# The last down projection of 256 tokens with tokens on partitions, normalised by bn_stats, its last 512 features in two PSUM tiles

## The chip, the cores and the metric

The kernel runs on one core of a Trainium2 chip. The metric is device time in microseconds from launch to end, taken as the median of several runs; three runs of the kernel before gave 1087.12, 1089.46 and 1090.7. One more execution was profiled, and every single duration below is from it.

A core has five engines with a queue of instructions each: TensorE (PE, with its weight loads shown as PEld), VectorE (DVE), ScalarE (ACT), GpSimd (POOL) and SyncE (SP, which here only issues DMAs). SBUF and PSUM have 128 partitions; TensorE writes PSUM alone, in banks of 512 fp32 values per partition.

## The reference

One layer of a hybrid trunk for 512 prompt tokens and 8 x 4 sample tokens, 544 in all, with 1024 features:

```
x = layer_norm(ALPHA * x + 0.5 * swiglu(x, ffn1), ln1)
proj = x @ w_in ; RWKV-7 heads and a short convolution ; mix = [y_rwkv, y_conv] @ w_out
x = layer_norm(ALPHA * x + mix, ln2)
y = layer_norm(ALPHA * x + 0.5 * swiglu(x, ffn2), ln3)

swiglu(x, wg, wu, wd) = (silu(x @ wg) * (x @ wu)) @ wd
layer_norm(x, g, b)   = (x - mean) * rsqrt(var + 1e-5) * g + b      # over the 1024 features
```

The hidden width of swiglu is 2816, which is 22 rows of 128. Only the very last line, the down projection `@ wd` of the second swiglu and its layer norm `ln3`, is touched by the change.

## The kernel before

**Layout.** Activations stand with features on partitions: `z` is 128 x 8 x 544, where `z[:, d]` holds features 128 d to 128 d + 127 of all tokens. `HALF` splits the tokens into 0 to 255 and 256 to 543. `z` holds ALPHA * x and collects the projection, so that it is the input of the norm (the residual and the products are doubled, and epsilon times four).

**Products.** Every factor is split into a high part in fp32r and a low part (the rest), and each product is three matmuls: high x high, high x low, low x high (`mm3`, L150 to L152). Weights are loaded by SP into a ring of `raw` tiles and split by ScalarE (L134) and VectorE (L135) into a ring of `hl` tiles (`wload`, `wsplit`); late in the kernel there are five raw tiles, six hl tiles and four half-size `hlb` tiles. PSUM has three banks named `mm` (`big()`) and five named `sm`.

**The second swiglu (`f2`).** The hidden rows are worked in `CHUNKS` of 4, 4, 4, 4 and 6. For all but the last chunk a Strassen-like scheme is used in both directions (`pairs`, `downs`, L547 to L549). The last chunk's six rows of hidden activations lie in `hhl` (high and low parts, 6 x 544), and its down projection is plain: `down(LAST, d, h)` computes the 128 features `d` for the tokens of half `h` from six weight blocks, adds the PSUM tile to `z` (L427), and adds the row into a running sum `s1` for the mean (`add_sum`). `main()` ends with the eight `down`s of the second half (288 tokens); their weights stay in SBUF, and `end()` is the eight `down`s of the first half (256 tokens) with the same weights.

**The end.** `layer_norm` of the second half is woven with `end()`: `weave` lets the norm, at each of its yields, hand a number of nanoseconds of matmul work to the other generator, scaled by `FILL["l3a"]`. The norm takes mean and variance over partitions with matmuls against a matrix of ones (L222), subtracts (L235), squares (L236), takes Ln and Exp on ScalarE (L255, L258), multiplies (L262), and applies gain and bias (L268). Once the first half's products are done, `layer_norm_end` normalises those 256 tokens in the same layout, in two groups of 128 tokens, and stores pairs of features as they come (lines L275 to L304). Nothing runs beside it.

**Order.** The program is written as generators; the framework's planner then orders each engine's instructions by the program's order and by when its own model thinks that they are ready, and puts in the waits. `tc.issue_after(x)` puts an instruction behind `x` in its engine's queue. Each engine's queue is in order on the chip, SP's too.

Of the kernel before, what the change touches and what calls it, by code (L numbers as in the profile page):

```python
# [12 lines left out]
F32 = mybir.dt.float32  # L13
F32R = mybir.dt.float32r
AF = mybir.ActivationFunctionType
OP = mybir.AluOpType
# [3 lines left out]
P = 128  # L20
D = 1024
KD = D // P
# [3 lines left out]
NSEQ = 8  # L26
TS = 4
T = TP + NSEQ * TS
B11, B21, B22, NT1, NT2, T3, T4 = range(7)
HALF = ((0, 256), (256, 544))  # L30
# [5 lines left out]
CHUNKS = ((0, 4), (4, 8), (8, 12), (12, 16), (16, 22))  # L36
LAST = len(CHUNKS) - 1
# [21 lines left out]


@with_exitstack
def body(ctx: ExitStack, tc: tile.TileContext, xT, gu1, wd1, win, wo_c, wo_0, wo_1, gu2, wd2, lora, vec, cst,
         sst, cstate, s0, y_o, wkvp_o, wkvs_o, shift_o, conv_o):
    nc = tc.nc
    PE, ACT, DVE, POOL = nc.tensor, nc.scalar, nc.vector, nc.gpsimd
    dma = nc.sync.dma_start

    def pool(st, name, side="left", **kw):
        return st.enter_context(tc.tile_pool(name=name, bufs=1, side=side, reuse_waits="tile", **kw))

    keep = pool(ctx, "keep")
    wp = pool(ctx, "wp")
# [14 lines left out]
    def col(v, i):  # L87
        return vc[:, v + i:v + i + 1]
# [4 lines left out]
    def sm():  # L93
        return ps.tile([P, 512], F32, name="sm", bufs=5)
# [105 lines left out]
    def weave(key, crit, *fill):  # L200
        bg.extend(fill)
        for need in crit:
            take(need * FILL[key])

    def drain(*fill):
        bg.extend(fill)
        take(1e9)
# [5 lines left out]
    def layer_norm(z, c0, c1, gcol, bcol, epsv, q, rs, s1, sink, table=None, hl2=None, both=False):  # L213
        n = c1 - c0
        pair = hl2 is None

        def mean_of(x, need):
            split(hl2[:, 0, :n], hl2[:, 1, :n], x)
            o = sm()
            yield need  # L220
            for i in range(2):
                PE.matmul(o[:, :n], onr, hl2[:, i, :n], start=(i == 0), stop=(i == 1))  # L222
            return o

        if pair:
            m = sm()
            PE.matmul(m[:, :n], ones, s1[:, :n], start=True, stop=False)
            PE.matmul(m[:, :n], ones, z[:, KD - 1, c0:c1], start=False, stop=True)
        else:
            m = yield from mean_of(s1[:, :n], 1300)  # L230
        yield 800 if pair else 300
        for j in range(4):
            zz = z[:, 2 * j:2 * j + 2, c0:c1]
            qq = q[:, 2 * j:2 * j + 2, :n]
            DVE.tensor_tensor(zz, zz, m[:, None, :n].to_broadcast([P, 2, n]), op=OP.subtract)  # L235
            sq = ACT.activation(qq, zz, AF.Square)  # L236
            if j == 0 and table == "ahead":
                tab = issue(sq, ACT.preload_act_table_set, "natural_log_exp_and_others")
            if pair:
                if j % 2:  # L240
                    DVE.tensor_tensor(q[:, 2 * j - 2:2 * j, :n], q[:, 2 * j - 2:2 * j, :n], qq, op=OP.add)
            elif j:
                DVE.tensor_tensor(q[:, 0:2, :n], q[:, 0:2, :n], qq, op=OP.add)
            yield 900 if pair else 1000
        if pair:
            v = sm()
            for i, j in enumerate((0, 1, 4, 5)):
                PE.matmul(v[:, :n], ones, q[:, j, :n], start=(i == 0), stop=(i == 3))
        else:
            DVE.tensor_tensor(q[:, 0, :n], q[:, 0, :n], q[:, 1, :n], op=OP.add)  # L250
            v = yield from mean_of(q[:, 0, :n], 900)
        yield 800 if pair else 600
        if table == "late":
            tab = issue(ACT.activation(warm, v[:, 0:1], AF.Copy), ACT.preload_act_table_set, "natural_log_exp_and_others")
        ln = ACT.activation(rs[:, :n], v[:, :n], AF.Ln, bias=epsv)  # L255
        if table:
            after(ln, tab)
        ACT.activation(rs[:, :n], rs[:, :n], AF.Exp, scale=-0.5)  # L258
        yield 1200 if pair else 600
        for d in range(0, KD, 2):  # L260
            zz = z[:, d:d + 2, c0:c1]
            DVE.tensor_tensor(zz, zz, rs[:, None, :n].to_broadcast([P, 2, n]), op=OP.mult)  # L262
            for e in (d, d + 1):
                x, g, b = z[:, e, c0:c1], col(gcol, e), col(bcol, e)
                if both and e > d:
                    DVE.tensor_scalar(x, x, g, b, op0=OP.mult, op1=OP.add)
                else:
                    ACT.activation(x, x, AF.Identity, scale=g, bias=b)  # L268
            sink(d, zz, c0, c1)
            yield 1600 if pair else 1700  # L270

    def layer_norm_end(z, gcol, bcol, epsv, q, rs, s1):

        m, o = sm(), sm()
        PE.matmul(m[:, :256], ones, s1[:, :256], start=True, stop=False)  # L275
        PE.matmul(m[:, :256], ones, z[:, KD - 1, 0:256], start=False, stop=True)
        for _ in range(3):
            PE.matmul(o[:, :256], ones, s1[:, :256], start=True, stop=True)
        cs = [slice(0, P), slice(P, 2 * P)]

        def two(x):
            return x[:, None, :].to_broadcast([P, 2, P])

        for c in cs:
            v = sm()
            for j in range(0, KD, 2):
                zz, qq = z[:, j:j + 2, c], q[:, j:j + 2, c]
                DVE.tensor_tensor(zz, zz, two(m[:, c]), op=OP.subtract)
                ACT.activation(qq, zz, AF.Square)
                for i in range(2):  # L290
                    PE.matmul(v[:, :P], ones, qq[:, i, :], start=(j + i == 0), stop=(j + i == KD - 1))
            ACT.activation(rs[:, c], v[:, :P], AF.Ln, bias=epsv)
            ACT.activation(rs[:, c], rs[:, c], AF.Exp, scale=-0.5)
        for n, c in enumerate(cs):
            for d in range(0, KD, 2):
                zz = z[:, d:d + 2, c]
                DVE.tensor_tensor(zz, zz, two(rs[:, c]), op=OP.mult)
                for e in (d, d + 1):
                    x, g, b = z[:, e, c], col(gcol, e), col(bcol, e)
                    if e % 2 or e == 6:  # L300
                        DVE.tensor_scalar(x, x, g, b, op0=OP.mult, op1=OP.add)
                    else:
                        ACT.activation(x, x, AF.Identity, scale=g, bias=b)
                dma(y_o[:, d:d + 2, c], zz)  # L304
        yield 0

    def to_x(spill):
        def sink(d, x, c0, c1):
# [3 lines left out]
        return sink  # L312

    def to_y(d, x, c0, c1):
        dma(y_o[:, d:d + 2, c0:c1], x)

    def add_sum(s1, z, d, c0, c1, top):
        n = c1 - c0
# [5 lines left out]
    class Ffn:  # L324
# [21 lines left out]

        def open_lnq(self):
            self.tst.close()
            return pool(self.tst, "lnq" + self.ph).tile([P, KD, 288], F32, name="lnq")

        def weights(self, key, src, n, pair=False):
            if key not in self.w:
# [313 lines left out]
        def main(self):  # L666
            self.open_tv()
            tv = self.inputs()
            self.raw, self.held, self.t = {}, [], 0
            self.todo, self.events = self.plan()  # L670
            z = self.z
            self.done, self.made = set(), set()
            for i, m in enumerate((3, 0, 1, 2) if self.nf > NEX else range(self.na)):
                if m >= self.nf:
                    yield from self.up(m, 0)
                yield from self.up(m, 1)
                next(tv)
                if i == 1 and self.nf < self.na:
                    for j, n in enumerate("gu"):
                        self.w[n, 3] = wload(self.gu[3, :, j, :])  # L680
                elif i in (1, 2):
                    self.t = (-12, -5)[i - 1]
                    self.feed()
            self.t = 0
            for _ in tv:
                pass
            for d in range(KD):
                ACT.activation(z[:, d], z[:, d], AF.Copy, scale=2.0 * ALPHA)
            for ci in range(LAST + 1):
                if ci:  # L690
                    yield from self.pairs(ci)
                if ci < LAST:
                    yield from self.downs(ci)
            for d in range(KD):
                yield from self.down(LAST, d, 1 - self.late)

        def end(self):
            return seq(*(self.down(LAST, d, self.late) for d in range(KD)))
# [780 lines left out]
    weave("l2b", ln2b, f2.first())  # L1479
    drain(f2.main())  # L1480
    lnq = f2.open_lnq()
    weave("l3a", layer_norm(z, *HALF[1], V_LN3G, V_LN3B, epsf, lnq, f2.lnr, f2.s1[1], to_y, "ahead", f2.hl2), f2.end())
    drain()
    drain(layer_norm_end(z, V_LN3G, V_LN3B, epsf, lnq, f2.lnr, f2.s1[0]))
    f2.close()


# [3 lines left out]
def _constants():  # L1491
# [15 lines left out]
    return c  # L1507


_OUTS = [("y", (P, KD, T)), ("wkvp", (P, 4, 64)), ("wkvs", (P, 4, NSEQ, 64)), ("shift", (P, 14, 9)),  # L1510
         ("conv", (P, 4, 2 + 2 * NSEQ))]


# [52 lines left out]
```

## Time and profile before

| what | us |
|---|---|
| median of three runs | 1089.46 |
| profiled execution, its own time | 1087.86 |
| its span, first to last instruction | 1086.1 |
| down rows of the last 288 tokens, from about | 1035.5 to 1054.3 |
| down rows of the first 256 tokens | 1054.3 to 1072.5 |
| normalisation of the first 256 tokens | 1072.5 to 1083.2 |
| last store, to the end of the span | 1083.2 to 1086.1 |

In the rows of the profile, times are microseconds from the start of the span. A row of a group has the line, engine, operation, output <- inputs, shapes and count, then busy time and the mean nanoseconds of one, then the idle time of the engine ahead of it and what ended that. A row of the timeline has start, length, engine, line and instruction. Matmuls are pipelined: what one costs is the distance between two starts, and not its length, which holds the way through the array too.

### The profile page before, as it was taken

How to read it: one execution, taken by the hardware profiler on the slowest of the kernel's cores; microseconds unless marked ns; L12 is line 12 of the kernel's file. 1: busy time of each engine (PE TensorE's matmuls, PEld its weight loads, DVE VectorE, ACT ScalarE, POOL GpSimd, SP SyncE). 2: the span in 40 equal slices, each digit the busy share in tenths (PEclk: the TensorE clock that was granted, in tenths of full speed). 3: DMA queues.
4: the chain of work that ended last, by engine and by line, in shares of the span. 5: the costliest groups of instructions: out<-in, count | busy, mean ns of one | idle time of the engine just before them, and what ended most of it. 6: DMA issues, size and time to landing. Idle time of an engine off the chain costs nothing.

```text
span 1086.1 us, 22868 instructions
## 1 busy us (share of the span) xinstructions
PE 1057.3 (97%) x9258; PEld 1018.5 (94%) x9258; DVE 846.2 (78%) x1576; ACT 588.7 (54%) x1095; POOL 177.5 (16%) x288
## 2 busy tenths in 40 slices
PE   9999999999999999999999999999999999999997
PEld 8999999999999988898889987999999999999996
DVE  7788888889675867775578558999889888888657
ACT  6655565555553677653445334667555565545425
POOL 0122220312200022141001200001312213121000
PEclk9999999999999999999999999999999999999999
DMA  8668595867854233243145625343857859677402
GB/s 280 138 124 191 121 217 132 177 156 148 187 117 154 80 114 84 59 111 85 42 141 185 146 78 178 117 136 78 184 152 153 196 119 211 154 156 177 122 1 83
DMA packets 99081, 148.88 MB, mean 137 GB/s; under 512 B 35232, under 2 KB 60576, under 8 KB 98976
## 3 DMA queue, kind: packets, MB, share of 16 engines
q1 hardware_dynamic: 71776, 111.25, 33.4%
q0 software_dynamic: 27200, 36.18, 22.0%
q8 instruction: 72, 1.18, 0.4%
q14 instruction: 33, 0.27, 0.1%
HBM read 128.74 MB, written 9.75 MB: 128 GB/s over the span
## 4 chain that ended last, share of the span: by engine, by line
PE 67%; issue 10%; DVE 9%; ACT 7%; DMA 6%; SPq 0%; POOL 0%; DVEq 0%; POOLq 0%; ACTq 0%
PE mm L150 7%; PE mm L547 7%; PE mm L151 7%; PE mm L548 7%; PE mm L549 7%; PE mm L152 7%; PE sm L549 5%; PE sm L548 5%; PE sm L547 5%; DMA raw<-in_gu 4%; ACT hl L134 3%; DVE hl L135 2%; PE sm L1047 1%; PE sm L150 1%; PE sm L151 1%
## 5 line engine op out<-in xcount | busy, mean ns | idle before, releaser
L135 DVE TENSOR_TENSOR hl<-raw,hl 128x1024 fp32r<-128x1024 f32 (+3 forms) x232 | 270.6, 1171 | 76.7 <-ACT hl L134 75.6
L134 ACT ACTIVATE hl<-raw 128x1024 fp32r<-128x1024 f32 (+3 forms) x232 | 232.0, 1013 | 90.4 <-DVE raw L514 40.9
L150 PE MATMUL mm<-xhl,hl 128*128 128x288 f32 (+1 forms) x736 | 218.8, 298 | 3.2 <-DVE z L1438 1.6
L151 PE MATMUL mm<-xhl,hl 128*128 128x288 f32 (+1 forms) x736 | 212.9, 289 | 0.3 <-DVE xhl L139 0.3
L152 PE MATMUL mm<-xhl,hl 128*128 128x288 f32 (+1 forms) x736 | 211.5, 288 | 0.1
L150 PEld LDWEIGHTS mm<-xhl,hl 128*128 128x128 f32 x736 | 138.0, 188 | 10.2 <-DVE z L1438 2.6
L151 PEld LDWEIGHTS mm<-xhl,hl 128*128 128x128 f32 x736 | 138.3, 188 | 2.5 <-issue 1.0
L152 PEld LDWEIGHTS mm<-xhl,hl 128*128 128x128 f32 x736 | 138.3, 188 | 1.1 <-DVE hl L135 0.5
L549 PE MATMUL sm<-xhl,hl 128*128 128x272 f32 x432 | 125.3, 290 | 0.0
L548 PE MATMUL sm<-xhl,hl 128*128 128x272 f32 x432 | 124.5, 288 | 0.0
L547 PE MATMUL sm<-xhl,hl 128*128 128x272 f32 x432 | 124.0, 287 | 0.0
L547 PE MATMUL mm<-tv,hl 128*128 128x272 f32 x288 | 83.3, 289 | 3.8 <-ACT cpb L608 2.0
L520 POOL DMA_DIRECT2D raw<-in_gu x36 | 43.4, 1206 | 258.1 <-DVE hlb L139 156.6
L549 PE MATMUL mm<-tv,hl 128*128 128x272 f32 x288 | 83.4, 290 | 0.0
L548 PE MATMUL mm<-tv,hl 128*128 128x272 f32 x288 | 83.1, 289 | 0.0
L547 PEld LDWEIGHTS sm<-xhl,hl 128*128 128x128 f32 x432 | 81.4, 188 | 0.0
L549 PEld LDWEIGHTS sm<-xhl,hl 128*128 128x128 f32 x432 | 81.3, 188 | 0.0
L548 PEld LDWEIGHTS sm<-xhl,hl 128*128 128x128 f32 x432 | 81.2, 188 | 0.0
L526 POOL DMA_DIRECT2D raw<-in_wd x32 | 39.3, 1481 | 249.1 <-DVE hlb L139 218.1
L547 PEld LDWEIGHTS mm<-tv,hl 128*128 128x128 f32 x288 | 54.3, 188 | 5.2 <-ACT cpb L608 3.1
L547 PE MATMUL mm<-hhl,hl 128*128 128x272 f32 x192 | 57.0, 302 | 0.7 <-DVE z L637 0.7
L547 PE MATMUL sm<-hhl,hl 128*128 128x272 f32 x192 | 55.9, 291 | 0.0
(393 smaller groups left out, 2785.5 us busy)
## 6 DMA issues: line engine op xcount, KB each, us to landing
raw<-in_gu SPq DMA_DIRECT2D x84, 512.0 KB, 4.6
raw<-in_gu POOLq DMA_DIRECT2D x36, 512.0 KB, 6.3
raw<-in_wd SPq DMA_DIRECT2D x32, 512.0 KB, 4.7
raw<-in_win SPq DMA_DIRECT2D x26, 512.0 KB, 3.7
raw<-in_wd POOLq DMA_DIRECT2D x32, 256.0 KB, 7.1
raw<-in_wd SPq DMA_DIRECT2D x16, 384.0 KB, 3.2
z<-cpb POOLq DMA_DIRECT2D x16, 272.0 KB, 9.4
z<-sv POOLq DMA_DIRECT2D x16, 272.0 KB, 6.5
```

Source lines behind the costliest of these rows:

```text
L134: ACT.activation(hl[:, 0, a:b], raw[:, a:b], AF.Copy)
L135: DVE.tensor_tensor(hl[:, 1, a:b], raw[:, a:b], hl[:, 0, a:b].bitcast(F32), op=OP.subtract)
L150: PE.matmul(out, wh, src[:, 0, k, c0:c1], start=(start and i == 0), stop=False)
L151: PE.matmul(out, wh, src[:, 1, k, c0:c1], start=False, stop=False)
L152: seen["fill"] = PE.matmul(out, wl, src[:, 0, k, c0:c1], start=False, stop=(stop and i == n - 1))
L520: POOL.dma_start(x.rearrange("p (s c) -> p s c", s=2), bass.AP(tensor=a11.tensor, offset=a11.offset, ap=[[2 * D, P], [P * 2 * D, 2], [1, 5 ...
L526: POOL.dma_start(four(x)[:, i], bass.AP(tensor=a11.tensor, offset=a11.offset, ap=[[DFF, P], [P * DFF, 2], [1, 256]]), accum_op=OP.add)
L547: PE.matmul(out, wh, src(0, i), start=(first and i == 0), stop=False, skip_group_check=True)
L548: PE.matmul(out, wh, src(1, i), start=False, stop=False, skip_group_check=True)
L549: PE.matmul(out, wl, src(0, i), start=False, stop=(i == n - 1), skip_group_check=True)
L1047: crit(PE.matmul(q[r0:r0 + m, o:o + nn], lhs, rhs, start=True, stop=True))
```

## The change

The down projection of the last six hidden rows is done in another layout for the first 256 tokens, and the norm of these tokens with it.

- The weights of the last chunk come as six tiles `wl[m]` of 128 hidden features x 1024 output features (512 KB each), in place of eight tiles of 128 x 768 (384 KB each).
- `down_wide` replaces the eight `down`s of the second half in `main()`: the same matmuls, of 288 columns; for the first four features rows the loop over `m` is the outer one and four PSUM tiles are open at once, for the other four rows it is as before. The split of the tiles from `m` = 4 on is queued behind the planner's held instructions.
- `end_wide` replaces `end()`. For each 128 tokens, `z` is transposed by TensorE into PSUM (eight transposes of 128 x 128 in fp32), and the products are added onto it with the activations as the stationary operand and the weights as the moving one, up to 512 columns wide. The first 128 tokens have two PSUM tiles of 512 features; the second 128 have one of 512 and two of 256.
- `layer_norm_rows` replaces `layer_norm_end`. With tokens on partitions, mean and variance come from bn_stats (per 256 features) and bn_aggr on VectorE, Ln and Exp run on one value per partition, and two passes of scalar_tensor_tensor apply (x - mean) * g and then * rs + b, by halves of 512 features, each with its store. The result is kept in the two tiles `hk` and `sv`, free by then.
- Gain and bias of `ln3` are loaded a second time, repeated on all partitions (`gb`, 1 MB), and an identity matrix (`idt`, 64 KB), into the space of `tv`; both are issued on SP behind the weights.
- The output has two parts: `y` for the second half in the old layout and `yt` for the first 256 tokens; the host puts them together.

```diff
-    def layer_norm_end(z, gcol, bcol, epsv, q, rs, s1):
...
+    def layer_norm_rows(o, y, g, b, epsv, st, out):
+        for q, c, n in o:
+            for i in range(0, n, 256):
+                j = 6 * ((c + i) // 256)
+                DVE.bn_stats(st[:, j:j + 6], q[:, i:i + 256])
+        mean, rs = st[:, 24:25], st[:, 26:27]
+        DVE.bn_aggr(st[:, 24:26], st[:, 0:24])
+        ACT.activation(rs, st[:, 25:26], AF.Ln, bias=epsv)
+        ACT.activation(rs, rs, AF.Exp, scale=-0.5)
+        for q, c, n in o:
+            DVE.scalar_tensor_tensor(y[:, c:c + n], q[:, :n], mean, g[:, c:c + n], op0=OP.subtract, op1=OP.mult)
+            if c + n in (512, 1024):
+                h = slice(c + n - 512, c + n)
+                DVE.scalar_tensor_tensor(y[:, h], y[:, h], rs, b[:, h], op0=OP.mult, op1=OP.add)
+                dma(out[:, h], y[:, h])
...
-            for d in range(KD):
-                yield from self.down(LAST, d, 1 - self.late)
+            if self.late:
+                for d in range(KD):
+                    yield from self.down(LAST, d, 0)
+            else:
+                yield from self.down_wide()
+
+        def down_wide(self):
...
+            def weights(m):
+                with ExitStack() as st:
+                    for e in self.held if m > 3 else ():
+                        st.enter_context(tc.issue_after(e.ins))
+                    return wload(wl[m])
...
+            def three(o, m, d, first, last):
+                hl, x = self.wm[m], self.hhl
+                for i, (v, y) in enumerate(((0, 0), (0, 1), (1, 0))):
+                    seen["fill"] = PE.matmul(o[:, :n], hl[:, v, P * d:P * d + P], x[:, y, m, c0:c1], start=(first and i == 0),
+                                             stop=(last and i == 2), skip_group_check=True)
+            os = [f() for f in (big, sm, big, sm)]
+            for m in range(n6):
+                self.wm.append(weights(m))
+                for d in range(4):
+                    three(os[d], m, d, m == 0, m == n6 - 1)
+                    if d % 2:
+                        yield 6 * (n / 2.4 + 3)
+            for d in range(4):
+                done(d, os[d])
+            for d in range(4, KD):
+                o = big() if d % 2 else sm()
+                for m in range(n6):
+                    three(o, m, d, m == 0, m == n6 - 1)
...
+                done(d, o)
+
+        def end_wide(self, gb, idt, st):
+            n6 = len(self.wm)
+            z, x = self.z, self.hhl
+            for t in range(2):
+                tok = slice(P * t, P * t + P)
+                o = [(f(), c, n) for f, c, n in (((big, 0, 512), (sm, 512, 256), (sm, 768, 256)) if t else
+                                                 ((big, 0, 512), (big, 512, 512)))]
+                where = [i for i, (_, _, n) in enumerate(o) for _ in range(n // P)]
+                for d in range(KD):
+                    q, c, n = o[where[d]]
+                    PE.matmul(q[:, P * d - c:P * d - c + P], z[:, d, tok], idt, start=(P * d == c), stop=False,
+                              is_transpose=True, skip_group_check=True)
+                yield 1500
+                for q, c, n in o:
+                    for m in range(n6):
+                        for i, (v, y) in enumerate(((0, 0), (0, 1), (1, 0))):
+                            seen["fill"] = PE.matmul(q[:, :n], x[:, y, m, tok], self.wm[m][:, v, c:c + n], start=False,
+                                                     stop=(m == n6 - 1 and i == 2), skip_group_check=True)
+                        if m % 2 or n == 512:
+                            yield 3 * n / 2.4 * (1 if n == 512 else 2)
+                layer_norm_rows(o, self.rows[t].rearrange("p a t -> p (a t)")[:, 0:D], gb[:, 0], gb[:, 1], epsf, st[:, t],
+                                yt_o[:, t])
...
-    weave("l3a", layer_norm(z, *HALF[1], V_LN3G, V_LN3B, epsf, lnq, f2.lnr, f2.s1[1], to_y, "ahead", f2.hl2), f2.end())
+    gb = f2.lp.tile([P, 2, D], F32, name="gb")
+    idt = f2.lp.tile([P, P], F32, name="idt")
+    st = f2.lp.tile([P, 2, 28], F32, name="st")
+    dma(idt, eye)
+    dma(gb, bass.AP(tensor=ln3.tensor, offset=ln3.offset, ap=[[0, P], [D, 2], [1, D]]))
+    weave("l3a", layer_norm(z, *HALF[1], V_LN3G, V_LN3B, epsf, lnq, f2.lnr, f2.s1[1], to_y, "ahead", f2.hl2),
+          f2.end_wide(gb, idt, st))
     drain()
-    drain(layer_norm_end(z, V_LN3G, V_LN3B, epsf, lnq, f2.lnr, f2.s1[0]))
...
+    a["wl"] = g["ffn2_wd"][0][CHUNKS[LAST][0] * P:].reshape(-1, P, D)
```

More of the change, by code (lines that the diff above doesn't have):

```diff
@@ L61, in body @@
 @with_exitstack
-def body(ctx: ExitStack, tc: tile.TileContext, xT, gu1, wd1, win, wo_c, wo_0, wo_1, gu2, wd2, lora, vec, cst,
-         sst, cstate, s0, y_o, wkvp_o, wkvs_o, shift_o, conv_o):
+def body(ctx: ExitStack, tc: tile.TileContext, xT, gu1, wd1, win, wo_c, wo_0, wo_1, gu2, wd2, wl, ln3, eye, lora, vec, cst,
+         sst, cstate, s0, y_o, yt_o, wkvp_o, wkvs_o, shift_o, conv_o):
     nc = tc.nc
@@ L270, in layer_norm @@
             yield 1600 if pair else 1700
-    def layer_norm_end(z, gcol, bcol, epsv, q, rs, s1):
[L274 to L305, printed above, removed]
@@ L314, in to_y @@
     def to_y(d, x, c0, c1):
-        dma(y_o[:, d:d + 2, c0:c1], x)
+        dma(y_o[:, d:d + 2], x)
     def add_sum(s1, z, d, c0, c1, top):
@@ L348, in open_lnq @@
             self.tst.close()
-            return pool(self.tst, "lnq" + self.ph).tile([P, KD, 288], F32, name="lnq")
+            self.lp = pool(self.tst, "lnq" + self.ph)
+            return self.lp.tile([P, KD, 288], F32, name="lnq")
         def weights(self, key, src, n, pair=False):
@@ L693, in main, with done @@
                     yield from self.downs(ci)
-            for d in range(KD):
-                yield from self.down(LAST, d, 1 - self.late)
+            if self.late:
[4 more added lines that the diff above has]
+        def down_wide(self):
+            m0, m1 = CHUNKS[LAST]
+            n6 = m1 - m0
+            c0, c1 = HALF[1]
+            n = c1 - c0
+            z = self.z
+            def weights(m):
[3 more added lines that the diff above has]
+                    return wload(wl[m])
+            self.wm = []
+            def done(d, o):
+                DVE.tensor_tensor(z[:, d, c0:c1], z[:, d, c0:c1], o[:, :n], op=OP.add)
+                add_sum(self.s1[1], z, d, c0, c1, KD)
+            def three(o, m, d, first, last):
[16 more added lines that the diff above has]
+                    three(o, m, d, m == 0, m == n6 - 1)
+                    if m % 2:
+                        yield 6 * (n / 2.4 + 3)
+                done(d, o)
@@ L1507, in _constants @@
     return c
-_OUTS = [("y", (P, KD, T)), ("wkvp", (P, 4, 64)), ("wkvs", (P, 4, NSEQ, 64)), ("shift", (P, 14, 9)),
+_OUTS = [("y", (P, KD, 288)), ("yt", (P, 2, D)), ("wkvp", (P, 4, 64)), ("wkvs", (P, 4, NSEQ, 64)), ("shift", (P, 14, 9)),
          ("conv", (P, 4, 2 + 2 * NSEQ))]
@@ L1536 @@
         a[name] = wo[:, :, k0:k1].reshape(KD // n, n, P, (k1 - k0) * P).transpose(0, 2, 1, 3).reshape(KD // n, P, D)
+    a["wl"] = g["ffn2_wd"][0][CHUNKS[LAST][0] * P:].reshape(-1, P, D)
+    a["ln3"] = np.stack([g["ln3_g"][0], g["ln3_b"][0]])
+    a["eye"] = np.eye(P, dtype=np.float32)
     a["lora"] = np.stack([np.concatenate([g["w_lora_up"][0], g["a_lora_up"][0]], 0), g["g_lora_up"][0]], 1)
@@ L1556 @@
     r = _run(nc, [arrays], core_ids=[0]).results[0]
-    y, wp, ws, sh, cv = (r["out_" + n] for n, _ in _OUTS)
-    y = y.transpose(2, 1, 0).reshape(T, D)
+    y, yt, wp, ws, sh, cv = (r["out_" + n] for n, _ in _OUTS)
+    y = np.concatenate([yt.transpose(1, 0, 2).reshape(2 * P, D), y.transpose(2, 1, 0).reshape(288, D)], 0)
     sh = sh.transpose(2, 1, 0).reshape(9, 14 * P)
```

## The prediction

> **What bounds the kernel now.** I read the page's head first, then the busy time by stretches over the last 78 us, then the chain that ended last, and then single rows for prices.
>
> ```profile
> span 1086.1 us, 22868 instructions
> PE 1057.3 (97%) x9258; PEld 1018.5 (94%) x9258; DVE 846.2 (78%) x1576; ACT 588.7 (54%) x1095; POOL 177.5 (16%) x288
> PE 67%; issue 10%; DVE 9%; ACT 7%; DMA 6%; SPq 0%; POOL 0%; DVEq 0%; POOLq 0%; ACTq 0%
> ```
>
> TensorE is busy for 97% of the span, so the average says only that matmul time counts. The change sits in the last 55 us; the stretches there (length, then busy time of PE, PEld, DVE, ACT, POOL, then granted clock, DMA share and GB/s) say more:
>
> ```profile
> 1031.70:1054.34 22.64, 22.64 (x171) 22.29 (x170) 12.84 (x26) 4.92 (x9) 0.00 (x0) 1.00 0.00 1
> 1054.34:1072.53 18.19, 18.19 (x151) 17.91 (x150) 14.43 (x29) 9.90 (x17) 0.00 (x0) 1.00 0.15 49
> 1072.53:1083.18 10.65, 6.25 (x42) 5.32 (x41) 8.50 (x27) 6.44 (x18) 0.00 (x0) 0.95 0.32 95
> 1083.18:1086.10 2.92, 0.00 (x0) 0.00 (x0) 0.00 (x0) 0.00 (x0) 0.00 (x0) 0.50 0.42 116
> ```
>
> Up to 1072.53 TensorE never rests: first the down rows of the last 288 tokens, then those of the first 256. After it come 10.65 us of normalisation and 2.92 us of store: 13.57 us in which no product is left to run. The chain (start, length, engine, tile, line) shows what they are made of:
>
> ```profile
> 1072.29 0.12 PE sm L151
> 1072.53 0.43 PE sm L275 x2
> 1074.79 2.06 PE sm L291 x16
> 1076.93 0.37 ACT cpb L292
> 1077.84 0.76 DVE z L297 x2
> ...
> 1082.92 0.26 DVE z L301
> ```
>
> Ones-matmuls for the mean, subtractions and squares for the variance, Ln and Exp, then a VectorE pass over all 1024 features of 256 tokens, which alone lasts from 1077.84 to 1083.18. A microsecond off this tail, or off TensorE before it, is a microsecond off the end.
>
> **The change, part by part.**
>
> *Products of the last 288 tokens (down_wide).* Still 8 rows x 6 weights x 3 = 144 matmuls of 288 columns; only the loops are exchanged for the first four rows. I cost this at nothing. The weights come as six tiles of 512 KB in place of eight of 384 KB: the same bytes, two issues fewer on SP. They are wanted faster, one tile per 12 matmuls. The cover is that the loads are early and the splits have time:
>
> ```profile
> 1008.14 14.83 SPq L117 DMA_DIRECT2D raw<-in_wd  x5
> 1023.85 2.71 SPq L355 DMA_DIRECT2D raw<-in_wd  x2
> DMA to landing us min/median/max: 3.1/3.2/4.0
> 1035.76 0.85 ACT L134 ACTIVATE hl<-raw 128x768 fp32r<-128x768 f32 x1 [0.42 <-PE sm L549]
> 1036.83 0.95 DVE L135 TENSOR_TENSOR hl<-raw,hl 128x768 fp32r<-128x768 f32 x1
> 1012.67 1.05 ACT L134 ACTIVATE hl<-raw 128x1024 fp32r<-128x1024 f32 x1
> 1012.21 1.22 DVE L135 TENSOR_TENSOR hl<-raw,hl 128x1024 fp32r<-128x1024 f32 x1
> 1053.54 0.30 PE L150 MATMUL sm<-hhl,hlb 128*128 128x288 f32 x1
> 1054.34 0.28 PE L150 MATMUL mm<-hhl,hl 128*128 128x256 f32 x1
> 1061.26 0.28 PE L150 MATMUL sm<-hhl,hl 128*128 128x256 f32 x1
> 1063.39 0.28 PE L150 MATMUL mm<-hhl,hl 128*128 128x256 f32 x1
> ```
>
> From 1053.54 to 1054.34 lie six matmuls of 288 columns: 0.133 us each, so a tile lasts 12 x 0.133 = 1.6 us. The loads shown are issued by 1026.6 (the first of the eight lies earlier still) and land 3.2 us after issue in the median of L117's, 4.0 at most; the last wide split waits for the last product of the pairs, until 1035.76. The rows run from about 1035.5, so tile 5 is wanted at 1035.5 + 5 x 1.6 = 1043.5; two last splits of 1.22 us on VectorE, beginning at 1036.83 where they do now and with one other split between, end near 1040. Slack is 3.5 us. A late tile would stop TensorE, since its queue is in order.
>
> ```profile
> 1056.01 0.40 PE L222 MATMUL sm<-hhl,ones 128*128 128x288 f32 x1
> ```
>
> *Start of the other half's norm.* Its first ones-matmul (L222) starts 1.7 us after the last 288-column row gives way at 1054.34; products of 256 columns fill this now. In the new order eight transposes (1.0 us, below) stand there, and what they leave open must be filled by products put ahead. Bounds 0 and 0.7 us idle; I take 0.2, nearer the present 0.1, since the same planner has products ready here.
>
> *Products of the first 256 tokens (end_wide).* 144 matmuls of 256 columns become 54 of 512 and 36 of 256. One row's 18 take 1063.39 - 1061.26 = 2.13 us, 0.119 each; 256/2.4 is 0.107, so some 0.012 is fixed. A 512 is then 0.226 (estimate from these rows). 144 x 0.119 = 17.1 before; 54 x 0.226 + 36 x 0.119 = 16.5 after: -0.65. Bounds -1.1 (nothing fixed) and 0 (a 512 costs two 256).
>
> *Sixteen fp32 transposes of 128x128*, which bring z into the PSUM tiles, replace the eight additions of L427 and lie on TensorE's path. The only transposes in the trace are of 64 columns:
>
> ```profile
> 581.90 0.22 PE L969 MATMUL sm<-cs,T 64*128 64x64 f32 x1
> 582.02 0.22 PE L969 MATMUL sm<-cs,T 64*128 64x64 f32 x1
> L291 PE MATMUL sm<-lnq,ones 128*128 128x128 f32 x32 | 4.1, 283 | 0.1
> ```
>
> Two lie between 581.90 and 582.02, 0.06 each, with one of the other 64 rows beside each. Twice the columns give 0.12; in the chain the 128-column fp32 records of L291 stand 2.06/16 = 0.129 apart. Bounds: 0.06 if the neighbours had taken half the time, 0.258 if a transpose were like a whole fp32 matmul (two such records). I take 0.12, which both the doubled row and the record give: 16 x 0.12 = +1.9 (1.0 to 4.1).
>
> The Trainium skill, page "TensorE: Matmul & The Clock Gate", section "Part 4: PE-mode transpose", reports about 275 ns for a 128x128 bf16 transpose inside a kernel. Estimated by it the sixteen would cost 4.4 us and the whole change would gain 2.9; the rows above, where starts lie 0.06 apart while a record lasts 0.22, suggest that such a figure is a length and not a distance.
>
> *First 128 tokens' norm* lies beside the second 128's products. VectorE loses eight L427 and six sums (each 0.34 from start to start, as L288 below: 4.8 us) and gains four bn_stats, a bn_aggr and four passes of 512, about 4.0 by the tail's prices. It was busy 14.43 of 18.19 us, so it does not become the bound. On VectorE and ScalarE these stand ahead of the other half's last pass, which in the worst order waits for the first products to end:
>
> ```profile
> L262 DVE TENSOR_TENSOR z<-z,cpb 128x576 f32<-128x576 f32 x4 | 2.9, 753 | 0.1
> L268 ACT ACTIVATE z<-z,vc 128x288 f32<-128x288 f32 x8 | 4.3, 614 | 0.8 <-DVE z L262 0.8
> ```
>
> TensorE is through the first 128 tokens at about 1054.3 + 1.0 + 8.1 + 1.0 (what the 18.19 us hold beside 17.1 of products) + 0.2 = 1064.6; VectorE's pass then takes 3.4 us, and ScalarE's eight follow, done near 1073, before its Ln for the second 128 near 1074.5. Slack 1.5 us: nothing.
>
> *gb (1 MB) and the identity* go out on SP behind the weights, once the last pair has released their space, into the stretch with DMA share 0.00; wanted 20 us later. Nothing.
>
> *The tail.* Gone: all of L275 to L304. In its place, counted from the last product's end, rows for the prices:
>
> ```profile
> L288 DVE TENSOR_TENSOR z<-z,sm 128x256 f32<-128x256 f32 x8 | 2.7, 416 | 0.9 <-PE sm L276 0.9
> 1015.34 0.44 DVE L584 SCALAR_TENSOR_TENSOR sv<-mm,sv 128x272 f32<-128x272 f32 x1
> 1006.66 0.69 DVE L513 TENSOR_TENSOR raw<-raw 128x512 f32<-128x512 f32 x1
> 1007.38 0.69 DVE L514 TENSOR_TENSOR raw<-raw 128x512 f32<-128x512 f32 x1
> 1079.08 0.35 ACT L292 ACTIVATE cpb<-sm,eps 128x128 f32<-128x128 f32 x1
> 1079.46 0.31 ACT L293 ACTIVATE cpb<-cpb 128x128 f32<-128x128 f32 x1
> out_y<-z SPq DMA_DIRECT2D x8, 128.0 KB, 1.9
> xsp<-z SPq DMA_DIRECT2D x4, 256.0 KB, 2.1
> ```
>
> L513 (512 values) and L135 (1024) give (1.22 - 0.69)/512 = 1.04 ns per value and 0.16 fixed; the three-operand L584 out of PSUM lies on that line. L514, which needs L513, starts 0.03 after it; independent ones (eight L288 in 2.74 us) start 0.08 before the last ends. So: wait 0.04; bn_stats of the last 256, unknown, as L288, 0.42 (0.2 to 0.84); bn_aggr of 24 values, unknown, 0.20 (0.18 to 0.35 as L301's 128); first pass over 512, 0.69; second 0.69; each with its 0.03: 2.13. Then two first passes of 256, +0.34 each, and the second 512, 0.72: 3.5. Ln and Exp (0.69 together for 128 columns, here one) lie beside the first pass of 512. The statistics of the first three quarters run under the last tile's 18 products, 2.1 us; that is what a tile of its own for the last 256 features allows. The store is 256 KB, and the rows say 0.2 more than the 2.92; with its twin in flight I take 3.2. Tail 6.7 against 13.57: -6.85 (bounds 6.2 and 8.0: -7.4 to -5.6).
>
> **Sum.** +0.2 - 0.65 + 1.9 - 6.85 = -5.4 us. The profiled execution took 1087.86 (its span 1086.1 and 1.8 around it), giving 1082.5. It lies 1.6 under the median of the runs, 1089.46; from the median I forecast 1084.0, 0.5% less.
>
> **The rivals.**
> *Transposes exposed in full.* If weight load and transpose do not overlap, each costs its record, as L291's 0.283: 16 x 0.283 = 4.5 in place of 1.9, net -2.8, 1086.7, within 0.3%. The page's 275 ns gives the same. For it: fp32 128-row weights were never alternated with a 128-column transpose here. Against: distances of 0.06. Chance 0.13.
> *VectorE late.* If the first 128's pass and the other half's last pass come behind one another later than I think, the statistics of the second 128 cannot start under the products: three bn_stats more in the tail (1.0) and up to two L262 (1.4): net -3.0, 1086.5. Against: 14.43 busy of 18.19. Chance 0.08.
> *Weights late: slower.* If tiles 2 to 5 were loaded only once the pairs had ended, one after the other, at 4.0 us each (L117's longest), and split in 1.05 and 1.22, tile 5 would be there at 1035.5 + 16 + 2.3 = 1053.8, 10.3 after it is wanted: net +4.9, 1094.4. It decides from 5.4 us of standstill, that is 8.9 us of delay past the planned split. Against: issue times of 1008 to 1026 with five raw buffers. Chance 0.07.
> *The change gains nothing*, by something not seen, either side of no change: 0.04.
>
> **How the numbers follow.** A measurement of this kernel tells about 0.3% (3.3 us) from no change. The forecast has 0.68, nearly all of it beyond 0.3%; its own range takes in part of the bounds of bn_stats, transposes and tail: 1081.5 to 1086.2. Exposed transposes and a late VectorE lie within 0.3% and raise the upper end to 1088; the lower end takes transposes of 0.06 and the shortest tail (-7.0, 1082.5) and 2 us for the runs' scatter, which spans 3.6. Faster 0.70, same 0.20, slower 0.10.
>
> **What would show it.** After: no idle TensorE between the pairs and the last product; 512-column matmuls 0.226 apart; 16 transposes near 0.12 apart; last product about 1 to 1.5 us later than 1072.5; then bn_stats, bn_aggr, five passes within 3.5 us, and the end 6.7 after the last product. A wait of TensorE on L135 or a DMA, transposes 0.25 apart, or a bn_stats far over 0.42 would make it wrong.

## The result and the profile after

The changed kernel has a median of 1085.56 us over nine runs, the kernel before 1089.46 over nine: 3.9 us less. The measured ratio is 0.9948 with a 95% interval of 0.9928 to 0.9968. It is not the ratio of these two medians, which is 0.9964; it would be 5.7 us of 1089.46, and its interval 3.5 to 7.8. Measured a second time, with the kernel before beside it, it was 0.9946 (0.9916 to 0.9977). The forecast was 5.4 us, so the runs show a gain, but can't say how near the forecast came. The profile can, by stretches. The profiled execution took 1085.56 us:

```profile
span 1083.8 us, 22658 instructions
PE 1056.7 (98%) x9178; PEld 1014.6 (94%) x9178; DVE 841.8 (78%) x1551; ACT 582.5 (54%) x1077; POOL 177.5 (16%) x288
```

I cut the end of both kernels at the same events: from the second start of the 288-token rows (four of their matmuls come earlier, between products of the pairs) to the first matmul for the first 256 tokens; from there to the VectorE instruction that waited for the last product; and from there to the end of the span. Busy time by stretches, of before:

```profile
1035.51:1054.34 18.83, 18.83 (x143) 18.67 (x142) 11.37 (x23) 1.51 (x2) 0.00 (x0) 1.00 0.00 1
1054.34:1072.57 18.23, 18.23 (x151) 17.93 (x150) 14.44 (x30) 9.90 (x17) 0.00 (x0) 1.00 0.15 49
1072.57:1086.10 13.53, 6.21 (x42) 5.29 (x40) 8.50 (x27) 6.44 (x18) 0.00 (x0) 0.85 0.34 99
```

and of after:

```profile
1038.15:1056.75 18.60, 18.60 (x142) 18.60 (x141) 9.83 (x19) 1.72 (x2) 0.00 (x0) 1.00 0.17 58
1056.75:1076.72 19.97, 19.93 (x112) 16.55 (x110) 15.34 (x29) 10.29 (x19) 0.00 (x0) 1.00 0.20 71
1076.72:1083.80 7.08, 0.00 (x0) 0.00 (x0) 3.64 (x7) 0.50 (x2) 0.00 (x0) 0.70 0.32 116
```

The tail went from 13.53 to 7.08 us, the products of the first 256 tokens from 18.23 to 19.97, the rows before them from 18.83 to 18.60: -6.45 + 1.74 - 0.23 = -4.94 us. The chain of after (start, length, engine, tile, line) shows the parts; L735 are the transposes, L741 the products, L277 bn_stats, L279 bn_aggr, L283 and L286 the two passes:

```profile
1056.91 0.87 PE mm L735 x8
1057.79 0.69 PE mm L741 x3
1058.48 0.35 PE sm L222
...
1059.33 7.43 PE mm L741 x32
...
1072.39 4.30 PE sm L741 x36
1076.72 0.44 DVE st L277
1077.18 0.27 DVE st L279
1077.48 0.81 DVE sv L283 x2
1078.29 0.25 issue
1078.54 0.74 DVE sv L286
1079.29 0.41 DVE sv L283
1079.72 0.75 DVE sv L286
```

The span is only 2.3 us shorter all the same. All of the changed part starts 2.4 to 2.6 us later than in the profile of before, though up to the last pairs each engine has the same instructions in the same order. Set against each other matmul by matmul, after loses 1.5, 1.4 and 1.6 us in three places where its granted clock fell, and gains back about 1.9 elsewhere. The stretches of after in question (before has 1.00 in both), then the third of these places alone, and one and the same group of four matmuls, in the chain first of before and then of after:

```profile
378.00:432.00 54.00, 49.92 (x355) 46.02 (x355) 35.37 (x62) 39.16 (x78) 13.02 (x53) 0.94 0.32 97
540.00:594.00 54.00, 51.44 (x513) 45.95 (x512) 43.19 (x96) 21.31 (x54) 5.81 (x14) 0.97 0.46 134
567.60:571.01 3.41, 3.41 (x13) 2.82 (x12) 1.28 (x3) 1.74 (x7) 0.00 (x0) 0.50 0.54 154
```

```profile
566.59 0.97 PE sm L984 x4
```

```profile
568.69 1.92 PE sm L1035 x4
```

Each place is a window of 3.4 us in which TensorE's clock was granted at half. The first profile of the changed kernel has three of them, the second two, the experiments between none and four, where the code is the same; so they are taken as scatter between executions. A whole run of this kernel can't show an effect of 1 us; a stretch at full clock shows 0.1.

### The profile page after: what moved, and what is told of

Its sections match the earlier page's. It is cut to its first block, busy times and chain, and to the rows that moved or that the text cites. A ratio compares the mean times of both kernels' runs of the same rounds, so it can differ in the third digit from the quotient of the medians.

```text
span 1083.8 us, 22658 instructions
## 1 busy us (share of the span) xinstructions
PE 1056.7 (98%) x9178; PEld 1014.6 (94%) x9178; DVE 841.8 (78%) x1551; ACT 582.5 (54%) x1077; POOL 177.5 (16%) x288
## 4 chain that ended last, share of the span: by engine, by line
PE 76%; DVE 9%; ACT 6%; issue 4%; DMA 3%; SPq 0%; POOL 0%; DVEq 0%; POOLq 0%; ACTq 0%
PE mm L530 9%; PE mm L531 8%; PE mm L532 8%; PE mm L150 7%; PE mm L151 6%; PE mm L152 6%; PE sm L532 6%; PE sm L530 6%; PE sm L531 6%; DMA raw<-in_gu 2%; ACT hl L134 2%; DVE hl L135 1%; PE sm L1098 1%; PE mm L741 1%; PE mm L705 1%
## 5 line engine op out<-in xcount | busy, mean ns | idle before, releaser
L150 PEld LDWEIGHTS mm<-xhl,hl 128*128 128x128 f32 x736 | 139.4, 190 | 10.3 <-DVE z L1489 2.6
```

Of the source, the lines that this page charges most:

```text
L150: PE.matmul(out, wh, src[:, 0, k, c0:c1], start=(start and i == 0), stop=False)
```

## The experiments

Every kernel was cut at the same three events. Lengths in us; the ratio is to the kernel before, run on the same chip; where there is none, one execution was looked at.

| kernel | 288-token rows | first 256 tokens | tail | ratio (95%) |
|---|---|---|---|---|
| before | 18.83 | 18.23 | 13.53 | |
| after | 18.60 | 19.97 | 7.08 | 0.9948 (0.9928 to 0.9968) |
| c_after, the same again | 18.60 | 19.90 | 7.01 | 0.9946 (0.9916 to 0.9977) |
| e1_weights_only | 18.60 | 18.24 | 13.68 | 0.9988 (0.9967 to 1.0009) |
| e2_one_tile | 18.61 | 19.83 | 7.15 | 0.9951 (0.9932 to 0.9970) |
| e3_no_transpose | 18.61 | 17.90 | 7.08 | 0.9918 (0.9887 to 0.9949) |
| e4_late_weights | 18.60 | 19.89 | 7.05 | 0.9959 (0.9933 to 0.9985) |
| e7_held_two | 18.78 | 19.91 | 7.09 | |
| e8_later_weights | 20.31 | 19.91 | 7.07 | 0.9983 (0.9965 to 1.0001) |
| e5_small_stores | 18.60 | 19.98 | 6.98 | |
| e6_spread_tail | 18.61 | 19.97 | 8.07 | 0.9949 (0.9932 to 0.9965) |
| e9_no_pool | 18.60 | 19.94 | 7.27 | |

A tail ends with the span, which the views give to 0.1 us, so it is good to 0.05. A stretch whose code is unchanged comes back within 0.1 us, and the tail of e1 within 0.15, whatever the execution's total. That is the measure for what follows. In the code shown, what stands behind a # is a note.

**The same again**

> The changed kernel once more, on the chip of its parts. Ratio to the kernel before 0.995 (0.993 to 0.997); at full clock the stretch from the first transpose to the end of the last product 19.9 us, the tail after it 7.1 us, as in its first profile. If its gain had come from anything ahead of the last pairs (it has the same instructions there), the gain would not repeat.

The gain repeats, and the three lengths within 0.1 us.

**The weights and the loops alone**

```diff
-                yield from self.down(LAST, d, 1 - self.late)
+                yield from self.down_wide()              # with wl, as in the change
...
+        def end_wl(self):                                # the old layout, with the tiles of wl
...
+                        seen["fill"] = PE.matmul(o[:, :256], self.wm[m][:, v, P * d:P * d + P], self.hhl[:, y, m, c0:c1],
...
-    weave("l3a", layer_norm(...), f2.end())
+    weave("l3a", layer_norm(...), f2.end_wl())
```

> The six wide weight tiles and the exchanged loops alone; the first 256 tokens in the old layout with the old norm. Theory (these cost nothing and give nothing; the whole gain is the end with tokens on partitions): products of the first 256 tokens 18.2 us, tail 13.6 us, ratio 1.000 within 0.002. Rival (part of the gain is the weights: two loads and four small splits fewer): 0.2% to 0.4% faster than before, with a shorter stretch between the pairs and the first 256 tokens.

Its stretches, cut at 1072.53:

```profile
1035.68:1054.28 18.60, 18.60 (x142) 18.60 (x141) 9.82 (x19) 1.72 (x2) 0.00 (x0) 1.00 0.00 1
1054.28:1072.53 18.25, 18.25 (x151) 17.95 (x150) 14.44 (x30) 9.90 (x17) 0.00 (x0) 1.00 0.15 49
1072.53:1086.20 13.67, 6.20 (x42) 5.29 (x40) 8.49 (x27) 6.44 (x18) 0.00 (x0) 0.86 0.34 98
```

Products and tail are those of before, the tail within 0.15. The rows of 288 tokens are 0.23 us shorter, as in the changed kernel, so this small part of the gain does belong to the tiles and loops. Most of it is one wait in the kernel before, where a matmul's weight load stood behind ScalarE's last split of hidden activations (`hhl`):

```profile
1037.72 0.19 PEld L150 LDWEIGHTS mm<-hhl,hl 128*128 128x128 f32 x1 [0.16 <-ACT hhl L138]
```

The starts on its two sides are 0.22 and 0.23 apart in place of 0.13. Neither the changed kernel nor e1 has a wait there: with the loop over `m` outside, the last hidden row is wanted later. All else of the gain is in the end with tokens on partitions. What the layout and bn_stats are each worth in the tail was not separated; they come together.

**One PSUM tile for the last 512 features**

```diff
-                o = [(f(), c, n) for f, c, n in (((big, 0, 512), (sm, 512, 256), (sm, 768, 256)) if t else
+                o = [(f(), c, n) for f, c, n in (((big, 0, 512), (sm, 512, 512)) if t else
```

> The last 512 features of the second 128 tokens in one PSUM tile in place of two. Theory (only a bn_stats of 256 more stands behind the last product, 0.34 us; one pass of 512 replaces two of 256, -0.2; 18 wide matmuls replace 36, -0.1): tail 7.2 to 7.4 us, products 19.8 us, ratio as the changed kernel's within 0.001. Rival (the two tiles are what makes the tail short): tail 8 us or more.

VectorE's statistics and second passes in the tail:

```profile
1081.05 0.76 DVE L277 BATCH_NORM_STATS2 st<-sm 128x6 f32<-128x256 f32 x2 [2.41 <-PE sm L741]
...
1083.47 1.41 DVE L286 SCALAR_TENSOR_TENSOR sv<-sv,st,gb 128x512 f32<-128x512 f32 x2
```

Two bn_stats stand behind the last product in place of one (0.76 against 0.43), but the passes need one instruction less and the products 0.07 to 0.14 less. The tail is 0.07 to 0.14 longer, the whole the same. The two tiles are not what shortened the tail.

**Without the transposes**

```diff
-                for d in range(KD):
-                    q, c, n = o[where[d]]
-                    PE.matmul(q[:, P * d - c:P * d - c + P], z[:, d, tok], idt, start=(P * d == c), stop=False,
-                              is_transpose=True, skip_group_check=True)
...
-                            seen["fill"] = PE.matmul(q[:, :n], x[:, y, m, tok], self.wm[m][:, v, c:c + n], start=False,
+                            seen["fill"] = PE.matmul(q[:, :n], x[:, y, m, tok], self.wm[m][:, v, c:c + n], start=(m + i == 0),
```

> The sixteen transposes left out, so the first 256 tokens lack the residual and the products of the other chunks. Theory (a transpose costs the distance of 0.11 us, in full on TensorE's path): products 19.9 - 1.75 = 18.2 us, tail unchanged at 7.1, 0.16% faster than the changed kernel. Rival 1 (a transpose costs its record, 0.28): 15.4 us. Rival 2 (hidden beside other work, since TensorE would wait for the other half's norm without them): 19.5 us or more.

```profile
1056.52:1074.42 17.90, 17.86 (x96) 14.76 (x94) 15.15 (x29) 10.01 (x19) 0.00 (x0) 1.00 0.18 63
```

19.90 to 19.97 became 17.90: sixteen transposes cost 2.0 us, 0.125 each. They are neither hidden nor exposed over their record. That record, in the changed kernel:

```profile
L735 PE MATMUL mm<-idt,z x12: 270/273/273, 1056.8 to 1067.5; 128*128 128x128 f32 x12
```

It lasts 0.273 us, and by the chain eight of them take 0.87, so that one starts 0.109 after another. The Trainium skill, page "TensorE: Matmul & The Clock Gate", section "Part 4: PE-mode transpose", has about 275 ns for a 128x128 bf16 transpose inside a kernel. The trace agrees with that as the length of one record, here in fp32; as a price for a row of transposes it would be 2.5 times too high, and the measurement decides.

**Late weights, twice**

```diff
+                    if m < 2:
+                        return wload(wl[m])
+                    if m == 2:
+                        self.mark = dma(mk, self.rows[1][0:1, 0, 0:4])        # e8: 540:544
+                    st.enter_context(tc.issue_after(self.mark.ins))
                     return wload(wl[m])
...
+            mk = dr.tile([1, 4], F32, name="mk")
```

> The loads of the weight tiles 2 to 5 wait on SP for the end of the pairs, by a store of four values of sv ahead of them. This is the prediction's slower rival made on purpose, with loads that follow one another on the queue and not one by one. Theory (the down rows have about 3 to 4 us of slack and no more, and TensorE's queue is in order): loads issued from 1039.5 us, tile 2 split near 1045.5 where it is wanted at 1041, tile 5 near 1051 where it is wanted at 1045.8; TensorE stands still 4.5 to 6.5 us in this stretch, and the gain is gone: ratio 0.998 to 1.002. Rival (products of other rows fill the gap): less than 2 us of standstill, ratio as the changed kernel's.

SP's queue and the last split of e4:

```profile
1033.16 0.30 SPq L697 DMA_DIRECT2D mk<-sv  x1
1033.52 2.19 SPq L117 DMA_DIRECT2D raw<-in_wl  x4
```

```profile
1044.16 1.22 DVE L135 TENSOR_TENSOR hl<-raw,hl 128x1024 fp32r<-128x1024 f32 x1
```

The values of sv that I had chosen as the mark are written earlier than I thought. The loads went out from 1033.5 us, tile 5 was split at 1045.4 and first used near 1047.0, and TensorE did not stop: 18.60. So the test was too mild to decide, but it shows that the loads may be that late for nothing. The second takes the last values written:

> As the late weights, with the mark behind the very last write of sv, some 9 us later: loads of tiles 2 to 5 issued from about 1042 us. In the run before, with loads from 1033.5 us, tile 5 was split at 1045.4 and first used near 1047.0, so 1.6 us of slack were left. Theory (no load is needed before that, but past it TensorE's queue stops): 9 us later is 7 us too late; standstill of TensorE 4 to 7 us between the pairs and the first 256 tokens, as far as the planner does not put other products ahead; ratio to before 0.999 to 1.003. Rival (the planner, which sees the late loads, fills the gap with the products of tiles 0 and 1 for the other rows): less than 3 us.

SP's queue, then TensorE's, of e8:

```profile
1042.98 0.30 SPq L697 DMA_DIRECT2D mk<-sv  x1
1043.34 1.77 SPq L117 DMA_DIRECT2D raw<-in_wl  x4
```

```profile
1046.15 0.56 PE L711 MATMUL sm<-hhl,hl 128*128 128x288 f32 x3
1048.16 0.53 PE L711 MATMUL mm<-hhl,hl 128*128 128x288 f32 x2 [1.45 <-ACT hl L134]
```

Loads issued some 10 us later than in e4, nearly 8 us later by the start of the rows, which lies at 1041.5 here and at 1039.6 there, stop TensorE once, for 1.45 us, and the stretch is 1.7 us longer. The rival of this experiment's expectation held: the order of instructions is another one, with products of tiles 0 and 1 for the other rows put ahead. What of the 0.3% between this ratio and the changed kernel's goes beyond the 1.7 us lies within the intervals.

**The splits queued later**

```diff
-                    for e in self.held if m > 3 else ():
+                    for e in self.held if m > 1 else ():
```

> The splits of the weight tiles 2 to 5, and not 4 and 5 alone, are queued behind the held instructions, so that three more splits run after the pairs. Theory (slack of 3.5 us in the prediction; by the trace of the changed kernel tile 3 is then ready near 1042.5 and wanted at 1042.6): no standstill of TensorE beyond 0.3 us. Rival (the slack is smaller than worked out): 1 us or more between the pairs and the first 256 tokens.

The stretch is 18.78, 0.18 us longer. Four splits run after the pairs in place of two, so two more, those of the tiles 2 and 3, and not three as the expectation counts. One weight load waits, for the split of tile 3:

```profile
1044.60 0.19 PEld L705 LDWEIGHTS mm<-hhl,hl 128*128 128x128 f32 x1 [0.16 <-DVE hl L135]
```

As the theory said, they use up the slack and no more.

**The tail: smaller stores, and work for other engines**

```diff
-            if c + n in (512, 1024):
-                h = slice(c + n - 512, c + n)
-                DVE.scalar_tensor_tensor(y[:, h], y[:, h], rs, b[:, h], op0=OP.mult, op1=OP.add)
-                dma(out[:, h], y[:, h])
+            h = slice(c, c + n)
+            DVE.scalar_tensor_tensor(y[:, h], y[:, h], rs, b[:, h], op0=OP.mult, op1=OP.add)
+            dma(out[:, h], y[:, h])
```

> The second pass and the store follow each PSUM tile: for the second 128 tokens the last pass is 256 wide and the last store 128 KB. Theory (a 256-wide pass ends 0.27 sooner than one of 512, though one pass more costs 0.08, and a 128 KB store takes 2.9 in place of 3.3): tail 6.5 us in place of 7.1. Rival (a third store on SP's queue costs what the smaller one saves): 7.1.

Its last two passes on VectorE:

```profile
1080.39 0.48 DVE L283 SCALAR_TENSOR_TENSOR sv<-sm,st,gb 128x256 f32<-128x256 f32 x1
1080.91 0.48 DVE L285 SCALAR_TENSOR_TENSOR sv<-sv,st,gb 128x256 f32<-128x256 f32 x1
```

The tail is 6.98, nothing gained. VectorE ends 3.87 us after its first instruction in the tail (1077.52 to 1081.39) against 3.75 in the changed kernel: its passes are the chain, so their sum counts, and cutting one in two adds an instruction's fixed part. The last store with what follows takes 3.1 in place of 3.3, less of a saving than the 0.4 that I had expected.

```diff
...
+            if len(o) == 3 and c == 0:
+                ACT.activation(y[:, h], y[:, h], AF.Copy, scale=rs)
+                POOL.tensor_tensor(y[:, h], y[:, h], b[:, h], op=OP.add)      # e9: DVE
+            else:
                 DVE.scalar_tensor_tensor(y[:, h], y[:, h], rs, b[:, h], op0=OP.mult, op1=OP.add)
+            dma(out[:, h], y[:, h])
```

> As the small stores, and the second pass of the second 128 tokens' first 512 features taken off VectorE: scaled by ScalarE, bias added by GpSimd. Theory (VectorE's passes set the end; 0.67 less there): tail 5.9 to 6.1 us, 1.1 us less than the changed kernel's, ratio to before 0.994. Rival (GpSimd's addition over 512 values is slower than VectorE's whole rest, 1.9 us, and sets the end, or slows VectorE beside it): tail 6.5 or more, end on POOL's store.

VectorE's second passes of 256 in e6 (ns min/median/max, first and last start), then by time the later of the two, GpSimd's addition and the issue of the last store:

```profile
L289 DVE SCALAR_TENSOR_TENSOR sv<-sv,st,gb x2: 473/978/1482, 1079.0 to 1079.4; 128x256 f32<-128x256 f32 x2
```

```profile
1079.44 1.48 DVE L289 SCALAR_TENSOR_TENSOR sv<-sv,st,gb 128x256 f32<-128x256 f32 x1
1079.30 1.34 POOL L287 TENSOR_TENSOR sv<-sv,gb 128x512 f32<-128x512 f32 x1 [71.56 <-ACT sv L286]
1081.58 0.40 SPq L290 DMA_DIRECT2D out_yt<-sv  x1
```

The tail grew to 8.07. One VectorE pass took its 0.47; the other, started 0.14 us after GpSimd's addition, took 1.48 and ended at 1080.92, 0.28 after GpSimd. Of the 0.99 that the tail is longer, VectorE's later end accounts for 0.34 (4.09 us after its first instruction in place of 3.75). The rest lies behind it. The three stores stand in order on SP's queue; the first one waits for GpSimd, goes out at 1080.66, and the others follow at 1081.11 and 1081.58, the last one 0.66 after VectorE had ended. So by these rows GpSimd's addition set the end through its store, and would have done so without holding VectorE.

> As the spread tail, with the bias of the first 512 features added by VectorE in place of GpSimd. There a VectorE pass over 256 values took 1.48 us beside GpSimd's addition of 1.34. Theory (VectorE is held while GpSimd works on SBUF): without GpSimd's addition the passes of 256 take 0.48 again, the tail is 7.0 us. Rival (the pass waited for something else, the scale by ScalarE on the same tile): a pass of over 1 us again.

```profile
L289 DVE SCALAR_TENSOR_TENSOR sv<-sv,st,gb x2: 479/480/480, 1084.9 to 1085.3; 128x256 f32<-128x256 f32 x2
```

With the addition on VectorE both passes take 0.48, on the same tiles and behind the same ScalarE step. GpSimd's addition is what held VectorE. The tail is 7.27, 0.3 more than expected. VectorE ends 3.85 us after its first instruction, for the addition takes 0.69 where the pass of 512 took 0.75 and there is one pass more, and the last of the three stores is issued 0.15 after that end, where the changed kernel takes 0.03; the wait for ScalarE is only 0.07. None of these beats the changed kernel.

## Why the prediction was right

The direction and the mechanism held, and the size nearly: 1084.0 was forecast and 1085.56 measured, and the stretches say -4.94 (-5.08 in the repeat) where the sum said -5.4. Part of this closeness is luck: the tail and the products gave 0.4 and 0.35 less than their terms, and 0.23 came from rows that were costed at nothing. Step by step:

- *Products of the last 288 tokens*, costed at nothing: they gain 0.23 us, which e1 places in the tiles and loops, and most of it in a wait of the kernel before that I hadn't looked at. The cover that I named is real: I had worked out 3.5 us of slack for tile 5, in the changed kernel its split ends at 1042.5 and it is first used near 1045.6, 3.1 later. In e7 two more splits fit with 0.18 us of loss.
- *Products of the first 256 tokens*, -0.65: a 512-column matmul takes 7.43/32 = 0.232 and not 0.226, a 256-column one 4.30/36 = 0.119 as before. 54 x 0.232 + 36 x 0.119 = 16.8 against 17.1, so -0.3. A 512 thus saves only some 0.007 against two 256, where I had put 0.012 on the part that doesn't grow with the width.
- *Transposes*, +1.9: 16 x 0.109 = 1.75 by their starts, 2.0 by leaving them out. The two rows that I went by gave 0.12 and 0.129 for one, against 0.109 and 0.125 here, so the distance was the right thing to price by, and the runs don't say which of the two rows was the better one.
- *Start of the other half's norm*, +0.2: what is left of +1.74 is 1.74 - 1.75 + 0.3 = 0.3 if the transposes are priced by their starts, and nothing if by leaving them out. It is not a standstill: TensorE is idle for 0.04 us of the stretch (19.93 busy of 19.97).
- *The first 128 tokens' norm* cost nothing. ScalarE's last pass of the other half ended at 1075.8, 1.7 us before it was wanted for Ln, and VectorE was idle for 1.70 us before the last bn_stats, as the two engines' rows of after show:

```profile
1071.55 4.26 ACT L268 ACTIVATE z<-z,vc 128x288 f32<-128x288 f32 x8 [2.55 <-DVE z L262]
```

```profile
1076.72 0.43 DVE L277 BATCH_NORM_STATS2 st<-sm 128x6 f32<-128x256 f32 x1 [1.70 <-PE sm L741]
```

- *gb and the identity*, nothing: e1, which doesn't load them, has the same 18.60 in the rows beside these loads.
- *The tail*, -6.85: -6.45. This is the term that was missed most. VectorE needs 3.75 us in place of 3.5: bn_stats is 0.43 as its stand-in, but bn_aggr is 0.26 and not 0.20, and a scalar_tensor_tensor pass is 0.75 for 512 values and 0.48 for 256, where the rows of other instructions that stood in for it gave 0.69 and 0.42. The store takes 3.3 in place of 3.2.

Of the rivals, transposes exposed over their record fell with the distance of 0.109, and a late VectorE with its idle 1.70 us. The slower one, late weights, was overpriced: I let the loads come one by one and TensorE's order stay as it was. When loads were held past the pairs on purpose, they followed one another on the queue, the planner put other products ahead, and it cost 1.7 us where I had written 10.3. Even held back so far, the kernel was not slower than before (0.9983).

## What to carry to other kernels

In a kernel whose main engine is busy 97% of the time, look at what runs when that engine has nothing left: here half of a 13.5 us tail could go, for 1.7 us of more TensorE work ahead of it. Price an instruction on TensorE by the distance of two starts, and one on VectorE with the operands that it will have. In a tail that is a chain on one engine, count the work of that engine first: here smaller pieces only added instructions to it, and a second engine held the first and kept the stores waiting behind its own.

## What the runs showed of the hardware

GpSimd's addition of 512 fp32 values held a VectorE pass over 256 for 1.48 us in place of 0.48. The pass ended 0.28 us after GpSimd, about what 256 values take at the prediction's 1.04 ns each (0.27, an estimate from its rows). The Trainium skill, page "SBUF — State Buffer", section "Who interferes with whom", says that a VectorE instruction with two SBUF inputs contends with a GpSimd instruction that reads SBUF, and the one that comes second blocks until the first is done; the trace agrees, 1.48 beside 1.34.

TensorE's granted clock fell to half for 3.4 us at a time while products ran, nearly always near 395, 428 or 567 us of the span, in some executions and not in others with the same code. With matmuls in the window it showed directly (1.92 us for four in place of 0.97). Why an execution gets more or fewer of these windows was not settled here.
